# Moving the first head's row maxima into the projection stage, and loading masks instead of computing them, in a one-core decoder layer

## The chip, the core and the metric

The kernel runs on one core of one Trainium2 chip. A core has a matrix engine (PE, with weight loads shown apart as PEld), a vector engine (DVE), an activation engine (ACT), a general engine (POOL) and a queue engine (SP) that only issues transfers here. Each engine works through its own instructions in order. The metric is the device time of the whole kernel in microseconds (us); the profile shows one execution of it, instruction by instruction.

## What is computed

One layer of a decoder over 16 learned meta tokens and 1,024 tokens, 1,024 channels each, in float32:

```python
h = rms_norm(h_res, pre_norm_g[i])
z = h @ w_in[i]                       # one projection, 7,328 columns
(pv, pg, cq, ckv, kr, mg, cu, cg, sbcx, sg, gl) = split_cols(z)
y_a = (pool_mixer(pv, ...) * silu(pg)) @ w_out_pool[i]
y_b = (mla_attention(cq, ckv, kr, ...) * silu(mg)) @ w_out_mla[i]
y_c = (conformer_conv(cu, ...) * silu(cg)) @ w_out_conf[i]
y_d = (short_conv(sbcx, ...) * silu(sg)) @ w_out_sc[i]
gts = sigmoid(gl + gate_bias[i])
m = gts[0] * y_a + gts[1] * y_b + gts[2] * y_c + gts[3] * y_d
h_res = h_res + rms_norm(m @ w_o[i], post_norm_g[i])
```

The attention branch has 8 heads. Queries are made from a normed 256-wide projection, keys and values from a normed 128-wide one; a rotary part of 32 channels is shared by all heads on the side of the keys. Scores are causal, and the softmax runs over all keys up to the query:

```python
s = jnp.einsum('bqhd,bkhd->bhqk', qb, k)
s = jnp.where(k_pos <= q_pos, s, -inf)
p = softmax(s)
o = einsum('bhqk,bkhd->bqhd', p, v)
```

## The kernel before, in words

Products in float32 are made from pairs of rounded halves, a high and a low part, with three matrix products each (high by high, high by low, low by high).

The kernel has three stages, and each is planned and issued by itself (`plan.flush()`, L1282, L1548, L1741).

*Projection.* The large products `h @ w_in` are made in the Strassen-Winograd manner: `unit` (L598) makes seven products of four 128-row blocks, 12 matrix instructions each, in the banks `ps_pa` to `ps_pd`, and writes its results to DRAM (`z_dram`, `th_dram`). `prep` (L567) loads weights, makes their sums on DVE and splits them on ACT and POOL. Beside this run four lanes of side tasks (L1232). A lane is a list of tasks in order, and `pump` (L1244), called after each product, records a step of each lane at the lane's pace. The second lane matters here: it makes the sums of the output weights that the last stage needs (`task_so`, L1200, four times: two loads of 512 KB, four additions and subtractions, two stores), then keys and values (`task_kv`), then queries for each half of the tokens (`task_q`, twice). All of this lane's larger tiles come from one group of four buffers, `t4` (L544); its small weights come from two buffers `w1`; its products go to the two `ps_x` banks. The third lane uses the four buffers `t2`.

*Attention* (from L1288). Head by head and for each half `c` of the queries (512 each), in the order of `seq` (L1492):
- `maxima(h, c)` (L1347) multiplies queries by keys, 128 queries at a time, adds the causal mask `maskS` to the last 128 columns, and reduces each block to row maxima in `mx` and then `mr`. PE transposes `mr`, and DVE multiplies it by a pattern of -1 (`negd`) into four extra rows of the query tile `qt`. The key tile `kt` has four rows of ones there, so that the score product subtracts the maximum by itself.
- `attend(h, c)` (L1380) makes the scores by key blocks with the keys as stationary operand, adds `maskT` where needed, takes the exponential on ACT, splits it on ACT and POOL (`pt`), and multiplies by the values (`vt`) into the bank `ps_o`, which is copied to `ol` (two buffers).
- `sums` and `head_out` normalise a head and gate it.
- `fills` (L1458) gives filler work: the output products of the other three branches (`ps_y`), 48 steps of 6 matrix instructions, each with a gate tile `th` (three buffers) and a weight tile `whl`.

At the head of this stage POOL fills `maskS`, `maskT`, `negd` and the ones rows of both `kt` tiles. `load_kv(0)` and the first two queries are loaded freely. What the loop loads further (L1524), head 1's keys and values included, stands in `plan.behind()`.

*Output.* The attention branch's output products, then `m @ w_o` in the Strassen-Winograd manner, the last norm, and the stores.

*What sets the order.* All code records operations; `Plan.flush` (L351) then plays them through a small model of the engines and issues them in the order that comes out. An operation is taken when its inputs are ready by the model, its tile has a free buffer, and no ready operation of its engine has a lower place. Places follow the order of recording, less `ahead(n)`; `behind()` (L267) lets an operation wait for the last PE operation recorded so far; `slow(n)` adds time to a load's modelled landing. Buffers of a group are given out in the order of recording. A tile of the second stage whose memory lies over tiles of the first waits for the last use of those (`lay_out`, L247). The modelled durations come from `cost` (L291). By the sizes of the tiles, the three `qt` buffers, the last part of `negd` and the first part of `kt0` lie over the four `t4` buffers, and `kt1` over the `t2` buffers.

The helper that issues every operation is one line (L349), so the profile's rows are told apart by tile names.

Of the kernel before, what the change touches and what calls it, by code (L numbers as in the profile page):

```python
# [21 lines left out]
F32 = mybir.dt.float32  # L22
# [26 lines left out]
LK, LR = 1088, 576  # L49

# [162 lines left out]
class Plan:  # L213
# [77 lines left out]
    def cost(eng, op, outs, ins, pow_):  # L291
# [163 lines left out]
def trunk_kernel(ctx, tc, a):  # L455
# [44 lines left out]

    z_dram = {}
# [15 lines left out]
    r_dram = [dram.tile([NT], F32, name=f"r{h}") for h in range(H)]  # L517

# [408 lines left out]

    def task_conv(m, c):
# [203 lines left out]

    def task_kv():
# [84 lines left out]
    def lane(*tasks):  # L1218
# [15 lines left out]
        lane(*[((), task_so, k) for k in range(KH)], (("ckv", "kr"), task_kv), (("cq0", "cq1"), task_q, 0), ((), task_q, 1),  # L1234
# [67 lines left out]
    for d in range(4):  # L1302
# [5 lines left out]
    maskS = qk.tile([P, P], F32, name="maskS")  # L1308
    POOL.memset(maskS, 0.0)
    POOL.affine_select(out=maskS, in_=maskS, compare_op=ALU.is_ge, fill=NEG,  # L1310
                       base=0, pattern=[[-1, P]], channel_multiplier=1)
    maskT = qk.tile([P, P], F32, name="maskT")
    POOL.memset(maskT, 0.0)
    POOL.affine_select(out=maskT, in_=maskT, compare_op=ALU.is_ge, fill=NEG,
                       base=0, pattern=[[1, P]], channel_multiplier=-1)

    negd = qk.tile([4, 4, P], F32, name="negd")
    POOL.memset(negd, -1.0)
    POOL.affine_select(out=negd, in_=negd, compare_op=ALU.is_equal, fill=0.0,
                       base=0, pattern=[[-1, 4], [0, P]], channel_multiplier=1)  # L1320
# [10 lines left out]
    for i in range(2):  # L1331
        POOL.memset(f(kt[i][QK:NA, 0, :L]), 1.0)

    def load_kv(h):
        e, k_, v_ = h % 2, kt[h % 2], vt[h % 2]
        k_ = k_[:, :, :L]
        ld(k_[:64], k_dram[h // 2][64 * e:64 * (e + 1)])
        if h == 0:
            ld(k_[64:96], kr_dram)
        if h == 1:  # L1340
            ld(k_[64:80], kr_dram[16:])
            ld(k_[80:96], kr_dram[:16])
# [4 lines left out]
    def maxima(h, c):  # L1347
# [7 lines left out]
        for r in range(4):  # L1355
# [5 lines left out]
            for b in range(nb):  # L1361
# [3 lines left out]
                if b == nb - 1:  # L1365
                    add(DVE, s[:, n - P:n], s[:, n - P:n], maskS)
# [410 lines left out]
```

## Time and profile before

| what | value |
|---|---|
| median of 3 runs | 1002.54 us (1001.99 to 1002.88) |
| the profiled execution | 1000.41 us |
| its span, first to last instruction | 998.7 us |
| PE busy | 972.7 us, 97% |
| DVE, POOL, ACT busy | 691.4, 690.7, 444.5 us |
| moved by DMA | 200.98 MB, mean 201 GB/s |

The profile gives each engine's busy time, the clock granted to PE, and for each wait what ended it. A row of the timeline is: start, length, engine, line, operation, tile written and tiles read, shapes, count, and in brackets the idle time before it with the operation that ended it. SPq rows are issues of transfers by SP. A row of a group ends with busy time, mean length in ns, and the idle time before it. The row of a wait is: total, times, longest.

### The profile page before, as it was taken

Reading aid. Unit: us, or ns where it says so; the run is one execution under the profiler, and the core shown is the slowest. Engines: PE = TensorE matmul, PEld = TensorE weight load, DVE = VectorE, ACT = ScalarE, POOL = GpSimd, SP = SyncE. Lnnn points to the kernel's source line nnn. Section 1 sums busy time; section 2 is a strip of 40 time slices with the busy share of each in tenths; the row PEclk is TensorE's granted clock in tenths of the full one; section 3 lists DMA queues with packets and bytes.
Section 4 is the critical chain, followed back from the end, with each engine's and each line's share of the span. In section 5 each row is a group of like instructions: output and inputs, shape, how many; then the busy total and the mean of one; then the engine's idle time right before and its main releaser. Section 6 shows DMA issues by size and latency. Waiting matters only on the chain.

```text
span 998.7 us, 15346 instructions
## 1 busy us (share of the span) xinstructions
PE 972.7 (97%) x5093; PEld 826.4 (83%) x5093; DVE 691.4 (69%) x1109; ACT 444.5 (45%) x898; POOL 690.7 (69%) x640
## 2 busy tenths in 40 slices
PE   9999998999999999999999999989999989999996
PEld 9999997889888887888877888868888878688885
DVE  6857979989789545635555464266687787799547
ACT  7643232443335544544534444116665446224631
POOL 6867586776566787776888587225679766656956
PEclk9999999999999999999999999989999999999998
DMA  7258664577877684677655647886649762683534
GB/s 250 76 186 282 213 205 150 164 233 254 261 249 231 227 283 149 212 232 216 187 167 170 205 146 242 295 225 214 190 139 272 194 192 75 242 248 112 187 108 168
DMA packets 133407, 200.98 MB, mean 201 GB/s; under 512 B 20034, under 2 KB 80569, under 8 KB 132560
## 3 DMA queue, kind: packets, MB, share of 16 engines
q1 hardware_dynamic: 124352, 183.22, 58.8%
q10 hardware_dynamic: 8656, 15.74, 4.2%
q8 instruction: 40, 0.66, 0.3%
q0 software_dynamic: 320, 1.05, 0.3%
q14 instruction: 39, 0.32, 0.1%
HBM read 127.31 MB, written 72.65 MB: 200 GB/s over the span
## 4 chain that ended last, share of the span: by engine, by line
PE 86%; POOL 4%; DVE 4%; issue 3%; DMA 2%; ACT 1%; SPq 0%; ACTq 0%; DVEq 0%; POOLq 0%
PE ps_pa L349 15%; PE ps_pb L349 14%; PE ps_pc L349 13%; PE ps_o L349 10%; PE ps_s L349 7%; PE ps_pd L349 7%; PE ps_y L349 7%; PE ps_u L349 7%; PE ps_x L349 4%; POOL S L349 1%; PE ps_w L349 1%; POOL A L349 1%; DMA kt<-kr 1%; DVE m L349 1%; POOL rs L349 1%
## 5 line engine op out<-in xcount | busy, mean ns | idle before, releaser
L349 PE MATMUL ps_pb<-T,S 128*128 128x512 f32 (+2 forms) x792 | 170.7, 359 | 0.0
L349 PE MATMUL ps_pa<-B,A 128*128 128x512 f32 (+2 forms) x792 | 170.0, 359 | 0.0
L349 POOL TENSOR_TENSOR S<-ss,S 128x512 fp32r<-128x512 f32 x84 | 113.7, 1366 | 59.8 <-ACT S L349 57.1
L349 PEld LDWEIGHTS ps_pa<-B,A 128*128 128x128 f32 x792 | 134.0, 188 | 22.1 <-issue 1.0
L349 PEld LDWEIGHTS ps_pb<-T,S 128*128 128x128 f32 x792 | 133.9, 189 | 21.8 <-issue 0.5
L349 POOL TENSOR_TENSOR pt<-p,pt 128x512 fp32r<-128x512 f32 (+4 forms) x112 | 103.5, 950 | 53.5 <-ACT pt L349 28.6
L349 POOL TENSOR_TENSOR A<-raw,A 128x512 fp32r<-128x512 f32 x84 | 112.6, 1350 | 38.9 <-ACT A L349 36.9
L349 DVE TENSOR_TENSOR u<-ps_pb,u 128x512 f32<-128x512 f32 (+2 forms) x66 | 40.3, 610 | 80.4 <-PE ps_pb L349 77.7
L349 DVE SCALAR_TENSOR_TENSOR ps_w<-conv,par,ps_w 128x512 f32<-128x512 f32 x116 | 87.2, 752 | 2.5
L349 PE MATMUL ps_pc<-T,S 128*128 128x512 f32 (+1 forms) x396 | 85.7, 360 | 0.0
L349 ACT ACTIVATE p<-ps_s 128x512 f32<-128x512 f32 (+4 forms) x112 | 49.6, 442 | 80.3 <-PE ps_s L349 35.8
L349 PE MATMUL ps_pd<-T,A 128*128 128x512 f32 (+2 forms) x396 | 84.7, 359 | 0.0
L349 PE MATMUL ps_y<-bo,whl 128*128 128x512 f32 x288 | 83.5, 410 | 0.1
L349 PE MATMUL ps_pc<-B,S 128*128 128x512 f32 (+1 forms) x396 | 83.4, 357 | 0.0
L349 ACT ACTIVATE S<-ss 128x512 fp32r<-128x512 f32 x84 | 50.3, 627 | 66.3 <-DVE ss L349 46.1
L349 PE MATMUL ps_o<-pt,vt 128*128 128x512 f32 (+4 forms) x336 | 73.8, 335 | 2.4 <-ACT ol L349 2.3
L349 PEld LDWEIGHTS ps_pd<-T,A 128*128 128x128 f32 x396 | 67.1, 188 | 10.7
L349 PEld LDWEIGHTS ps_pc<-T,S 128*128 128x128 f32 x396 | 66.5, 189 | 11.1 <-issue 0.7
L349 PEld LDWEIGHTS ps_pc<-B,S 128*128 128x128 f32 x396 | 66.8, 188 | 10.6
L349 PE MATMUL ps_s<-qt,kt 100*128 100x512 f32 (+4 forms) x336 | 68.0, 332 | 0.7 <-DVE qt L349 0.7
L349 PEld LDWEIGHTS ps_o<-pt,vt 128*128 128x128 f32 (+1 forms) x336 | 52.8, 174 | 15.6 <-ACT ol L349 3.6
L349 PEld LDWEIGHTS ps_s<-qt,kt 100*128 100x128 f32 (+1 forms) x336 | 55.7, 182 | 11.8 <-issue 0.9
(265 smaller groups left out, 1913.4 us busy)
## 6 DMA issues: line engine op xcount, KB each, us to landing
raw<-in_w_in_dram SPq DMA_DIRECT2D x52, 512.0 KB
th<-th SPq DMA_DIRECT2D x32, 512.0 KB
th<-z ACTq DMA_DIRECT2D x60, 256.0 KB
v<-vhl SPq DMA_DIRECT2D x16, 384.0 KB
qt<-q SPq DMA_DIRECT2D x16, 384.0 KB
vt<-v SPq DMA_DIRECT2D x8, 768.0 KB
bo<-bo SPq DMA_DIRECT2D x6, 1024.0 KB
kt<-k SPq DMA_DIRECT2D x8, 520.0 KB
```

Source lines behind the costliest of these rows:

```text
L349: getattr(self.handle[o["eng"]], o["op"])(*map(real, o["args"]), **{k: real(v) for k, v in o["kw"].items()})
```

## The change

- The row maxima of head 0 are made in the projection stage: a task `task_first(c)` for each half loads the head's keys and queries from DRAM into `t4` buffers, makes a mask, multiplies and reduces as before, in the `ps_x` banks, and leaves the result in a small tile `mrs`. `maxima` of head 0 in attention only transposes it.
- The masks, the -1 pattern and the ones rows are made once in the projection stage by `task_consts`, stored in DRAM, and loaded at the head of attention.
- In the second lane `task_kv` and `task_q` come first, then `task_consts`, `task_first` twice, and `task_so` last.
- At the first turn of the attention loop, the loads of head 1's keys and of the next query are not `behind` any more; head 1's values stay so. The filler's loads are `behind`, except for the first tile.
- `head_out` of all heads but the last is recorded 450 places later (`ahead(-450)`).
- One tile `mxs`, filled once, takes the place of the `mx` tiles filled for each head and half.
- The model's durations are altered: ACT on PSUM, memsets and `affine_select`, POOL's operations, and DVE's `scalar_tensor_tensor` with source and target in PSUM.

```diff
+FIRST = 1
...
+        psum = any(isinstance(v, View) and v.buf.psum for v in outs + ins)
         if eng == "ACT":
-            return 200 + 0.83 * n, 0
+            return (160 + 0.857 * n if psum else 200 + 0.83 * n), 0
+        if op in ("memset", "affine_select"):
+            return (60 if op == "memset" else 180) + 0.85 * n, 0
         if eng == "POOL":
-            return (500 + 140 * n if pow_ else 80 + 2.4 * n), 0
-        psum = any(isinstance(v, View) and v.buf.psum for v in outs + ins)
+            return (500 + 140 * n if pow_ else 180 + 2.2 * n), 0
         if op == "reciprocal":
             return 150 + 8.5 * n, 0
-        return 142 + (1.2 if op == "scalar_tensor_tensor" and not psum else 1.07) * n, 0
+        both = psum and outs[0].buf.psum
+        return 142 + (1.2 if op == "scalar_tensor_tensor" and (both or not psum) else 1.07) * n, 0
...
+    mrs = const.tile([P, FIRST, 2, 4], F32, name="mrs")
...
+    mask_dram = [dram.tile([P, P], F32, name=f"mask{i}") for i in range(2)]
+    negd_dram = dram.tile([4, 4, P], F32, name="negd")
+    ones_dram = dram.tile([4, L], F32, name="ones4")
...
+    def causal(mask, sign=1):
+
+        POOL.memset(mask, 0.0)
+        POOL.affine_select(out=mask, in_=mask, compare_op=ALU.is_ge, fill=NEG,
+                           base=0, pattern=[[-sign, P]], channel_multiplier=sign)
+
+    def task_consts():
+
+        for i in range(2):
+            mask = w1([P, P], name="mask")
+            causal(mask, 1 - 2 * i)
+            ld(mask_dram[i], mask)
+        t = t4([4, L], name="kone")
+        POOL.memset(t, 1.0)
+        ld(ones_dram, t)
+        t = t4([4, 4, P], name="negd")
+        POOL.memset(t, -1.0)
+        POOL.affine_select(out=t, in_=t, compare_op=ALU.is_equal, fill=0.0,
+                           base=0, pattern=[[-1, 4], [0, P]], channel_multiplier=1)
+        ld(negd_dram, t)
+        yield
+
+    def k_rows(k_, h, part):
+
+        e = h % 2
+        ld(k_[:64], part(k_dram[h // 2][64 * e:64 * (e + 1)]))
+        if h < 2:
+            for r in range(2):
+                ld(k_[64 + 16 * r:80 + 16 * r], part(kr_dram[16 * (r ^ e):16 * (r ^ e) + 16]))
+
+    def row_maxima(c, mx, q_, k_, mask, bank):
+
+        for r in range(4):
+            nk = NM + P * (4 * c + r + 1)
+            nb = -(-nk // 512)
+            w_ = -(-nk // nb)
+            w_ += w_ % 2
+            n0 = 0
+            for b in range(nb):
+                n = min(w_, nk - n0)
+                s = bank()
+                PE.matmul(s[:, :n], q_[:, P * r:P * (r + 1)], k_[:, n0:n0 + n], start=True, stop=True)
+                if b == nb - 1:
+                    add(DVE, s[:, n - P:n], s[:, n - P:n], mask)
+                DVE.tensor_reduce(mx[:, r, b:b + 1], s[:, :n], axis=AX.X, op=ALU.max)
+                n0 += n
+            yield
+
...
+    def task_first(c):
+
+        n = NM + 512 * (c + 1)
+        for h in range(FIRST):
+            k_ = t4([QK, L], F32R, name="k0")[:, :n]
+            k_rows(k_, h, lambda x: x[:, 0, :n])
+            q_ = t4([QK, 512], F32R, name="q0")
+            ld(q_, q_dram[c][h][:, 0])
+            mask = w1([P, P], name="mask")
+            causal(mask)
+            yield
+            mx = tp.tile([P, 4, 3], F32, name="mx")
+            POOL.memset(mx, NEG)
+            yield from row_maxima(c, mx, q_, k_, mask, bank)
+            DVE.tensor_reduce(mrs[:, h, c], mx, axis=AX.X, op=ALU.max)
...
-        lane(*[((), task_so, k) for k in range(KH)], (("ckv", "kr"), task_kv), (("cq0", "cq1"), task_q, 0), ((), task_q, 1),
+        lane((("ckv", "kr"), task_kv), (("cq0", "cq1"), task_q, 0), ((), task_q, 1), ((), task_consts), ((), task_first, 0), ((), task_first, 1),
+             *[((), task_so, k) for k in range(KH)],
              ): 0.9,
...
-    maskS = qk.tile([P, P], F32, name="maskS")
-    POOL.memset(maskS, 0.0)
...
+    mxs = at.tile([P, 2, 2, 4, 3], F32, name="mxs")
+    POOL.memset(mxs, NEG)
+    maskS, maskT = (qk.tile([P, P], F32, name=n) for n in ("maskS", "maskT"))
     negd = qk.tile([4, 4, P], F32, name="negd")
...
-    for i in range(2):
-        POOL.memset(f(kt[i][QK:NA, 0, :L]), 1.0)
+    for t, src in ((maskS, mask_dram[0]), (maskT, mask_dram[1]), (negd, negd_dram),
+                   *((kt[i][QK:NA, 0, :L], ones_dram) for i in range(2))):
+        ld(t, src)
...
-        mx = at.tile([P, 4, 3], F32, tag="mx", bufs=2, name="mx")
-        POOL.memset(mx, NEG)
...
+        if h < FIRST:
+            mr = mrs[:, h, c]
+            for _ in range(4):
+                yield
+        else:
+            mx = mxs[:, h % 2, c]
+            yield from row_maxima(c, mx, q_[:QK, 0], k_[:QK, 0], maskS, lambda: bank("s"))
+            mr = at.tile([P, 4], F32, tag="mr", bufs=2, name="mr")
+            DVE.tensor_reduce(mr, mx, axis=AX.X, op=ALU.max)
...
-                whl = wtile(fp, wname, d, 0)
                 th = fp.tile([P, NT], F32, tag="th", bufs=3, name="th")
-                ld(th, th_dram[8 * gi + d])
+                with plan.behind() if d + bi else nullcontext():
+                    whl = wtile(fp, wname, d, 0)
+                    ld(th, th_dram[8 * gi + d])
...
-        with plan.behind():
+        with plan.behind() if i else nullcontext():
             if i + 2 < len(seq):
                 load_q(*seq[i + 2])
             if c == 0 and h + 1 < H:
                 load_kv(h + 1)
+                if i == 0:
+                    with plan.behind():
+                        load_v(1)
...
-        with plan.ahead(300 if h == H - 1 else 0):
+        with plan.ahead(300 if h == H - 1 else -450):
```

More of the change, by code (lines that the diff above doesn't have):

```diff
@@ L13 @@
 import re
-from contextlib import ExitStack, contextmanager
+from contextlib import ExitStack, contextmanager, nullcontext
 import concourse.bass as bass
@@ L1336, in load_kv, with load_v @@
         k_ = k_[:, :, :L]
-        ld(k_[:64], k_dram[h // 2][64 * e:64 * (e + 1)])
-        if h == 0:
-            ld(k_[64:96], kr_dram)
+        k_rows(k_, h, lambda x: x)
         if h == 1:
-            ld(k_[64:80], kr_dram[16:])
-            ld(k_[80:96], kr_dram[:16])
+            return
+        load_v(h)
+    def load_v(h):
+        v_ = vt[h % 2]
         v = v_dram[h // 4][h % 4]
```

26 lines of the change are left out of this document (removed).

## The prediction

> **What bounds the kernel now.** I read the page first, for the busy shares and the granted clock; then the windows, to find where the matrix engine (PE) loses time; then the chain and the timeline there.
>
> ```profile
> span 998.7 us, 15346 instructions
> PE 972.7 (97%) x5093; PEld 826.4 (83%) x5093; DVE 691.4 (69%) x1109; ACT 444.5 (45%) x898; POOL 690.7 (69%) x640
> PEclk9999999999999999999999999989999999999998
> ```
>
> PE is the bound: busy in 97% of the span, so 26 us idle. The clock row is nearly flat, with a dip about two thirds of the way. The windows (span, each engine's busy time, granted clock, DMA share, GB/s) show both losses at one place, where the projection ends and attention begins:
>
> ```profile
> 50.00:170.00 120.00, 117.61 (x854) 111.53 (x851) 94.62 (x142) 39.66 (x83) 84.89 (x65) 1.00 0.65 210
> 565.00:645.00 80.00, 79.60 (x357) 65.29 (x356) 36.08 (x46) 32.18 (x57) 47.74 (x43) 1.00 0.68 215
> 650.00:660.00 10.00, 9.34 (x43) 7.56 (x43) 6.93 (x15) 0.00 (x0) 0.61 (x4) 1.00 0.84 280
> 660.00:665.00 5.00, 4.63 (x23) 3.21 (x22) 4.97 (x15) 3.54 (x9) 2.49 (x3) 1.00 1.01 215
> 665.00:670.00 5.00, 1.86 (x7) 1.78 (x8) 1.85 (x7) 0.22 (x2) 1.23 (x4) 0.74 1.01 262
> 670.00:675.00 5.00, 5.00 (x19) 4.25 (x18) 2.26 (x6) 0.60 (x1) 0.00 (x0) 0.50 0.14 36
> 675.00:680.00 5.00, 5.00 (x17) 3.97 (x17) 1.98 (x5) 3.52 (x7) 2.25 (x2) 0.74 0.31 105
> ```
>
> Idle: 0.66 + 0.37 + 3.14 = 4.2 us. Half clock: 5 x (0.26 + 0.50 + 0.26) = 5.1 us of lost pace. Together 9.3 us; the projection's last 80 us, for comparison, lose 0.4. The chain there (start, length, what) and the timeline's rows say why:
>
> ```profile
> 641.08 2.72 PE ps_pc L349 x12
> 658.44 8.73 DMA kt<-kr
> 643.64 0.71 PE L349 MATMUL ps_s<-kt,qt 96*128 96x144 f32 x4
> 645.02 12.00 PE L349 MATMUL ps_y<-bo,whl 128*128 128x512 f32 x52
> 648.47 1.87 POOL L349 MEMSET kt<- 4x1040 f32 x2
> 656.07 1.80 DVE L349 TENSOR_REDUCE mx<-ps_s 128x1 f32<-128x144 f32 x5
> 657.85 0.55 SPq L349 DMA_DIRECT2D kt<-k  x1
> 668.14 0.78 PE L349 MATMUL ps_s<-kt,qt 96*128 96x144 f32 x2 [3.22 <-DMA kt<-kr]
> ```
>
> The first head's maxima for its first half are multiplied from 643.64 on but reduced only at 656. PE spends 12 us on filler (the branches' output products). The planner had set the reductions so late because it prices each ones-row memset of `kt` at 80 + 2.4 x 1040 = 2.58 us; the row says 1.87 for two. Head 1's keys are loaded `behind` the last of those maxima, so their DMAs leave at 657.85. Filler and head 0's scores run out at 664.9, and the rotary rows land 8.73 us after issue. The filler is not lost work; the 9.3 us are.
>
> **The change, part by part.** *Maxima of head 0.* Their products have 144+272+400+528 columns for the first half and 656+784+912+1040 for the second, 4,736 in all. At 2.72 us per 12 x 512 that is 2.1 us of PE, which moves and doesn't vanish: 0. DVE takes 14 reductions and 8 mask adds along:
>
> ```profile
> L349 DVE TENSOR_REDUCE mx<-ps_s x112: 300/500/634, 656.1 to 837.3; 128x1 f32<-128x264 f32 x16, 128x1 f32<-128x328 f32 x16, 128x1 f32<-128x392 f32 x16, 128x1 f32<-128x456 f32 x16
> L349 DVE TENSOR_TENSOR ps_s<-ps_s,maskS 128x128 f32<-128x128 f32 x64 | 18.3, 290 | 7.6 <-PE ps_s L349 7.5
> PE ps_x L349 <- POOL rs L349: 2.6, 2, 2.0
> ```
>
> 14 x 0.50 + 8 x 0.29 = 9.3 us, hidden in the projection's last 80 us, where DVE works 36. But PE takes its queue in order, and each product needs one of two `ps_x` banks back from DVE. The nearest row for a side task that is planned too early is the wait for `rs`, 2.6 us; bounds 0 and +2.6. I take +1.0: the 14 steps are short and DVE is half idle.
>
> *Masks, -1 rows and ones rows.* POOL's work for them in front of attention goes (1.87 for the ones rows, and six small instructions). In its place stand, in the projection, four instructions for the two stored masks, four for the masks of the early maxima, three for the row patterns, and four stores; then, for attention, five loads. With eight loads for the early maxima and one more for the rotary rows, that is 18 more DMAs on SP, at 0.3 to 0.6 us of issue (the `kt<-k` row has 0.55): some 8 us of a queue that is mostly empty. POOL's 48 us of 80 leave room. 0, as long as the loads come early; that is the first rival. The 16 memsets of `mx` become one. Five of them held POOL's queue, and with it the splits of the exponentials, behind DVE:
>
> ```profile
> POOL mx L349 <- DVE mr L349: 13.9, 5, 7.6
> PE ps_s L349 <- DVE mr L349: 2.8, 1, 2.8
> PE ps_o L349 <- ACT ol L349: 2.3, 3, 1.6
> 810.02 5.42 DVE L349 TENSOR_TENSOR m<-m,th 128x512 f32<-128x512 f32 x1
> 800.00:820.00 20.00, 16.81 (x86) 13.92 (x86) 16.92 (x28) 7.42 (x20) 14.99 (x18) 0.94 0.70 230
> ```
>
> *Keys and queries of head 1 not behind; its values, and all filler tiles but the first, behind; heads' outputs 450 places later.* Head 1's keys can then leave as soon as their place is free. It lies over the side tasks' `t2` buffers, last read at 612.54 by the store quoted below. That takes the 3.14 us wait and the half clock away. What is late next is the short chain transpose, multiplication by -1 rows, first scores (the 0.66 us above), now with two filler steps and head 1's maxima beside it. I leave 1.0 of the 9.3. The 450 places work on the `ol` buffers (2.3 us of PE waits now): normalising later can hold `ol` longer, or spare DVE a blocked queue. Attention's other big loss is 800 to 820, 3.2 us idle and 0.06 x 20 = 1.2 of clock, behind one DVE addition of 5.42 us. A new order can lose it or repeat it elsewhere: bounds -4.4 and +4.4, and I take 0, as no row says which.
>
> *Prices in the planner.* They cost nothing themselves and alter the order. The convolution's step was priced 142 + 1.07 x 512 = 690 ns and is now 756:
>
> ```profile
> L349 DVE SCALAR_TENSOR_TENSOR ps_w<-conv,par,ps_w 128x512 f32<-128x512 f32 x116 | 87.2, 752 | 2.5
> ```
>
> A plan nearer to the chip should not wait more; counted with the bounds above.
>
> *The output weights' sums (`task_so`) go to the end of their lane.* This frees 40 to 124 us, where PE idles 2.4 us of 120; bounds 0 and -2.4, I take -0.7. What it costs at the other end depends on when the lane ends:
>
> ```profile
> 39.52 1.72 SPq L349 DMA_DIRECT2D so<-in_w_o_dram  x2
> 52.63 0.34 SPq L349 DMA_DIRECT2D so<-in_w_o_dram  x1
> 66.76 0.86 SPq L349 DMA_DIRECT2D so<-in_w_o_dram  x1
> 72.94 0.93 SPq L349 DMA_DIRECT2D so<-in_w_o_dram  x2
> 85.65 0.44 SPq L349 DMA_DIRECT2D so<-in_w_o_dram  x1
> 101.18 0.33 SPq L349 DMA_DIRECT2D so<-so  x1
> 122.50 1.70 SPq L349 DMA_DIRECT2D so<-so  x2
> 129.16 0.92 SPq L349 DMA_DIRECT2D kcs<-in_trig_dram  x2
> 607.52 0.61 SPq L349 DMA_DIRECT2D q<-qr  x1
> 612.54 0.34 SPq L349 DMA_DIRECT2D bo<-cgt  x1
> 614.05 0.57 SPq L349 DMA_DIRECT2D kt<-k  x1
> ```
>
> The lane lives in four `t4` buffers. Its keys got their last buffer at 129.2, after the sums; without them the fourth buffer is there at 66.8. So keys and queries shift by some 62 us, and the last query is stored at about 546 instead of 607.5. The early maxima follow: a load at up to 8.7 us, then 14 blocks at up to 1.3 us (estimate: product, add, reduction, hand-overs), so buffers come free at about 563 and 574. Then the sums, two at a time. The third took 72.9 to 101.5, 28 us, the fourth 85.7 to 124.2, 38 us. In the emptier stretch after 565 (POOL busy 60% against 71%) I put 24 us each, and 5 for a store to land: 574 + 2 x (24 + 5) = 632. Attention's first query, its first keys and the -1 rows lie over the same buffers; loaded then, they are there before PE is done at about 645 (641.08 + 2.72 now, and 2.1 of products moved in, less the small change). So 0 in the forecast, with 10 us to spare.
>
> **Sum.** -9.3 + 1.0 (chain left) + 1.0 (early maxima) + 0 - 0.7 = -8.0 us, on the profiled execution's 1000.4 (span 998.7 and 1.7 around it): 992.4. The median of the runs shown is 2.1 above that execution, so 994.5.
>
> On the size of the half clock the Trainium skill, "TensorE: Matmul & The Clock Gate", Part 1, has a rule: about 3.4 us of sustained work restores full speed. By that rule the dip would cost 1.7 us instead of 5.1 and the sum would be -4.6; the granted clock here says three windows long, so the row decides and the rule gets no chance of its own.
>
> **Rivals.** *1, slower: the sums end too late.* If they keep their old pace of 38 us, the last buffer is free at 574 + 2 x (38 + 5) = 660, and the load of head 0's queries and keys adds 5 more. PE is done at 645 and has only two filler steps (6 x 0.227 us each, 2.7 us in all), since the other filler tiles now wait behind attention. Idle 660 + 5 - 645 - 2.7 = 17 us, and the half clock again 5: +22 against -9.3, some 1015. It decides from about 647 on: 4 us idle and 5 of clock eat the gain. At 652 the time is 1008. For it: the old pace and the DMA share, 0.68 already, to which four sums add 8 MB. Against: the emptier POOL, and a stretch after 625 without weights to prepare.
> The Trainium skill, "SBUF — State Buffer", section on the two separate sides, gives this rival a cause: an addition on DVE with two SBUF inputs and a POOL instruction that reads SBUF shut each other out for a whole instruction. The 5.42 us addition above agrees in kind, though it is longer than one instruction of POOL.
>
> *2, the wait only moves.* With more loads ahead of attention, head 1's keys or another tile land late again, and 4 us idle with 5 of clock stand elsewhere: 1002. For it: a DMA share of 1.01 at 660 to 670. Against: 30 us between 614 and 645 in which the queue can load.
>
> *3, attention gains too.* The 800 to 820 loss goes as well: 994.5 - 4.4 = 990. For it: the 13.9 us of POOL behind `mx`, gone by construction. Against: the 5.42 us addition has no tie to it.
>
> **How the numbers follow.** Forecast (with its own bounds, 991 to 999) 0.54; rival 3 0.10; rival 2 0.10; rival 1 0.26. A change under 0.2% (2 us) can't be told from none here. Faster: 0.54 + 0.10 + 0.02 of rival 2 = 0.66. Same: 0.06 of rival 2. Slower: 0.26 + 0.02 = 0.28. The range 989 to 1008 leaves out the far end of rival 1, about 0.13, and 0.04 below; the forecast alone is 991 to 999.
>
> **What would show it.** Right: the maxima's products of head 0 under `ps_x` before 645; `kt<-k` of head 1 issued before 645; clock 1.00 through 640 to 680; the block of 52 filler products broken up. The sums' last store before 635 and head 0's `kt<-k` before 640 clear rival 1. Wrong: PE idle around 645 on a DMA of `qt`, `kt` or `negd`, with `so<-so` stores just before; new waits of `ps_x` on DVE over 2.6 us in all; waits of `ps_o` on `ol` beyond 2.3.

## The result and the profile after

| | kernel before | changed kernel |
|---|---|---|
| median, us | 1002.31 (1001.99 to 1002.88) | 991.15 (990.20 to 991.64) |
| profiled execution, us | 1000.4 | 990.85 |
| its span, us | 998.7 | 989.0 |

The ratio is 0.9887, with an interval from 0.9870 to 0.9904: 1.1% faster. The time lies inside the predicted range, 3.4 us below the predicted 994.5. The total came out near, but its largest term did not.

The head of the changed kernel's page:

```profile
span 989.0 us, 15388 instructions
PE 969.4 (98%) x5095; PEld 824.6 (83%) x5095; DVE 696.8 (70%) x1109; ACT 444.0 (45%) x898; POOL 692.7 (70%) x630
```

PE idles 19.6 us of the span; before it was 26.0. The windows of the changed kernel (span, busy time of PE, PEld, DVE, ACT, POOL, then granted clock, DMA share, GB/s):

```profile
50.00:170.00 120.00, 117.99 (x874) 113.07 (x873) 84.34 (x135) 46.10 (x98) 76.45 (x62) 1.00 0.56 168
565.00:645.00 80.00, 79.62 (x358) 65.35 (x356) 47.09 (x56) 30.52 (x48) 54.52 (x41) 1.00 0.79 246
645.00:650.00 5.00, 1.16 (x6) 0.52 (x4) 1.46 (x3) 0.72 (x1) 0.00 (x0) 1.00 1.01 423
650.00:655.00 5.00, 5.00 (x19) 4.23 (x20) 3.31 (x12) 2.73 (x6) 2.61 (x4) 0.53 1.01 408
655.00:660.00 5.00, 5.00 (x22) 4.00 (x20) 0.00 (x0) 1.77 (x6) 1.75 (x4) 0.78 1.04 339
660.00:680.00 20.00, 20.00 (x117) 17.03 (x116) 13.93 (x39) 12.58 (x30) 12.43 (x14) 1.00 0.71 227
```

The hole at the start of attention is still there. It now lies at 645 to 650 instead of 660 to 670: 3.84 us idle and 5 x (0.47 + 0.22) = 3.45 us of pace lost to half clock, 7.3 together, where the prediction had counted 9.3 before. Only 2.0 of the 8.3 us came. The timelines of the changed kernel's PE, DVE and POOL (start, length, engine, and in brackets the idle time before and what ended it) show the wait that took the old one's place:

```profile
643.69 1.29 PE L353 MATMUL ps_pc<-B,S 128*128 128x512 f32 x5
645.40 0.47 PE L353 MATMUL ps_s<-kt,qt 96*128 96x144 f32 x2 [0.20 <-PE ps_s L353]
649.25 0.45 PE L353 MATMUL ps_s<-kt,qt 96*128 96x400 f32 x1 [3.38 <-DVE z L353]
648.50 0.69 DVE L353 TENSOR_TENSOR z<-ps_pc,u 128x512 f32<-128x512 f32 x1 [8.23 <-DMA th<-z]
649.23 1.28 DVE L353 TENSOR_TENSOR qt<-ps_s,negd 4x512 fp32r<-4x512 f32 x2
639.34 0.76 POOL L353 DMA_DIRECT2D th<-z  x1 [11.35 <-ACT z L353]
```

The projection's last gate block needs one of three `z` buffers back. The store out of that buffer was issued on POOL at 639.34 and lands some 9 us later, so DVE stands 8.23 us, until 648.50. Behind the waiting instruction on DVE's queue is the multiplication of head 0's maxima by `negd`, and behind that all scores of attention. The DMA share is 1.01 to 1.04 there; POOL's four gate stores took 6.7 to 9.0 us to land, in the kernel before 3.7 to 6.7. The SP queue of the changed kernel says why the transfers bunch:

```profile
617.75 0.43 SPq L353 DMA_DIRECT2D maskS<-mask  x1
618.23 0.42 SPq L353 DMA_DIRECT2D maskT<-mask  x1
619.85 0.27 SPq L353 DMA_DIRECT2D negd<-negd  x1
622.16 2.49 SPq L353 DMA_DIRECT2D kt<-ones  x2
626.03 0.54 SPq L353 DMA_DIRECT2D kt<-k  x1
631.42 1.25 SPq L353 DMA_DIRECT2D kt<-kr  x2
```

The five small loads stand ahead of head 0's keys, and the queue stops among them. Its waits from 610 to 640 (total, times, longest) name the gate stores `th<-z`, from which these loads read nothing:

```profile
SPq L353 <- DMA th<-z: 10.2, 4, 4.8
```

The trace's record of the semaphores shows what ties them. The 678 transfers that SP and ACT issue take eight semaphores in turn to tell of their landing, and one starts only when the one that had its semaphore before has landed. Four stores of ACT landed at 622.14, 624.34, 626.01 and 631.40; the four loads that have their semaphores next (the two of the ones rows, `kt<-k` and the first `kt<-kr`) left at 622.16, 624.40, 626.03 and 631.42. POOL's stores have semaphores of their own. This belongs to the program, and the planner knows of it: `fits` in `Plan.flush` lets no transfer of SP or ACT start while the eighth before it is in flight.

`kt<-k` leaves at 626.03; before it left at 614.05. After 631 everything goes at once.

So where did the 9.7 us of span go? The output stage starts here, in the kernel before and in the changed one:

```profile
868.10 2.10 PE L349 MATMUL ps_u<-boM,whl 128*128 128x512 f32 x8
```

```profile
859.29 2.09 PE L353 MATMUL ps_u<-boM,whl 128*128 128x512 f32 x8
```

The projection ended at 641.08 + 2.72 = 643.8 and now ends at 643.69 + 1.29 = 645.0: +1.2, though 2.1 us of products moved in. Attention took 868.1 - 643.8 = 224.3 and now takes 859.3 - 645.0 = 214.3: -10.0, of which 2.1 are those products, 2.0 the smaller hole, and 5.9 lie in its later part. The rest of the span gave 0.9. The later part of attention in the windows, before and after:

```profile
720.00:800.00 80.00, 79.30 (x427) 66.22 (x426) 61.95 (x149) 46.33 (x103) 66.97 (x71) 1.00 0.71 197
800.00:870.00 70.00, 64.61 (x330) 52.24 (x330) 54.90 (x101) 32.06 (x73) 46.88 (x46) 0.98 0.50 171
```

```profile
720.00:800.00 80.00, 80.00 (x424) 66.27 (x422) 56.73 (x141) 41.10 (x93) 62.29 (x61) 1.00 0.77 214
800.00:860.00 60.00, 58.61 (x300) 47.23 (x300) 47.36 (x91) 25.82 (x59) 40.43 (x37) 1.00 0.54 173
```

Idle and clock before: 0.70 + 5.39 + 0.02 x 70 = 7.5 us. After: 1.39. These 6.1 us are the term that the prediction took as 0.

### The profile page after: what moved, and what is told of

The parts are those of the page before. It is cut to its first block, busy times and chain, and to the rows that moved or that the text cites. A ratio compares the mean times of both kernels' runs of the same rounds, so it can differ in the third digit from the quotient of the medians.

```text
span 989.0 us, 15388 instructions
## 1 busy us (share of the span) xinstructions
PE 969.4 (98%) x5095; PEld 824.6 (83%) x5095; DVE 696.8 (70%) x1109; ACT 444.0 (45%) x898; POOL 692.7 (70%) x630
## 5 line engine op out<-in xcount | busy, mean ns | idle before, releaser
L353 POOL TENSOR_TENSOR A<-raw,A 128x512 fp32r<-128x512 f32 x84 | 114.6, 1370 | 39.2 <-ACT A L353 37.6
L353 POOL TENSOR_TENSOR pt<-p,pt 128x512 fp32r<-128x512 f32 (+4 forms) x112 | 105.6, 967 | 49.4 <-PE ps_s L353 31.5
L353 PE MATMUL ps_y<-bo,whl 128*128 128x512 f32 x288 | 87.1, 409 | 0.0
L353 PE MATMUL ps_pc<-B,S 128*128 128x512 f32 (+1 forms) x396 | 86.4, 359 | 0.0
L353 PE MATMUL ps_s<-qt,kt 100*128 100x512 f32 (+4 forms) x336 | 70.5, 333 | 0.3 <-DVE qt L353 0.3
L353 DVE TENSOR_TENSOR z<-ps_pc,u 128x512 f32<-128x512 f32 (+1 forms) x66 | 40.2, 609 | 37.3 <-PE ps_pc L353 27.3
```

Source lines behind the costliest of these rows:

```text
L353: getattr(self.handle[o["eng"]], o["op"])(*map(real, o["args"]), **{k: real(v) for k, v in o["kw"].items()})
```

## The experiments

The theories: *the pile-up* says that the hole at the start is caused by the order of the loads, so that removing one wait there shows another until the loads are spread. *The shut-out* says that the later part gained because a DVE instruction with both inputs in SBUF no longer stands for several us behind POOL. Against them stand the prediction's mechanism, the early maxima, and the single edits: places, prices, order of the sums. The kernel before had medians of 1000.2 to 1001.8 us beside these runs; the ratios are against it. The changed kernel itself was measured only in the first comparison (991.15, ratio 0.9887), so a difference of about 2 us from it by medians tells nothing.

**The last gate block without the wait for a `z` buffer.** The result goes into the block's own temporary tile.

```diff
-    def halves_of(n, each, store):
+    def halves_of(n, each, store, own=None):
...
-            z = up.tile([P, n], F32, tag="z", bufs=3, name="z")[:m, :nj]
+            z = tmp if (i, j) == own else up.tile([P, n], F32, tag="z", bufs=3, name="z")[:m, :nj]
...
-        return halves_of(512, each, lambda i, j, t: (POOL if g == 30 else ACT).dma_start(half(th_dram[g + i], j), t))
+        return halves_of(512, each, lambda i, j, t: (POOL if g == 30 else ACT).dma_start(half(th_dram[g + i], j), t),
+                         (0, 1) if g == 30 else None)
```

> The changed kernel, but the projection's very last gate block is made in the tile u2, which nobody needs any more, so that it doesn't wait for one of the three z buffers. Theory A (DVE stands at 645 to 648.5 in front of this block because a gate store issued at 639 has not landed, and head 0's multiplication by -1 rows is queued behind it): PE's 3.4 us wait and the 6.8 us of half clock after it both go, 3.4 + 3.4 = 6.8 us, so about 984.5. Rival (the DMA queues are simply full at 640 to 660, and keys or queries would be late anyway): PE waits for a tile of qt or kt in the same place, and the time stays at 989 to 991.

Measured 992.82 us, ratio 0.9893 to 0.9931. The 3.38 us wait is gone, and PE's waits in attention begin with

```profile
PE ps_y L353 <- DMA whl<-w_out_pool: 3.7, 1, 3.7
```

at 653: a filler's weights. From 645 to 660 PE loses 4.45 us idle and 3.45 of pace, no less than in the changed kernel (3.84 and 3.45). The named wait was only the first of several, and the time is above both expectations.

**Without the -450.** Heads' outputs are recorded in their old places.

```diff
-        with plan.ahead(300 if h == H - 1 else -450):
+        with plan.ahead(300 if h == H - 1 else 0):
```

> The changed kernel with the heads' outputs recorded at their old place (0 instead of -450). Attention after its first 35 us lost 7.3 us less than before; theory B gives this to the later place of the outputs: then the loss comes back, about 998. Rivals (prices, the single mx tile, filler spared at the start): within 1.5 us of 991.

Measured 998.10 us, 0.9950 to 0.9974: 7 us of the gain are lost. The start is as in the changed kernel; the loss lies at 807. The longest of DVE's rows there, PE's second wait in attention, and the product that it holds up:

```profile
802.41 4.57 DVE L353 TENSOR_TENSOR op<-ol,rb 64x512 f32<-64x512 f32 x2
```

```profile
PE ps_s L353 <- DMA whl<-w_out_sc: 2.8, 1, 2.8
807.65 0.27 PE L353 MATMUL ps_s<-ident,mr 128*4 128x128 f32 x1 [2.82 <-DMA whl<-w_out_sc]
```

One of the two multiplications took 3.96 us. The profile names the weights' load as releaser, but the matrix product that waits is the transpose of `mr`, which the row-maximum chain behind that DVE row feeds; `mr` is reduced at 806.90.

**The old prices in the changed kernel.** The planner's cost function is that of the kernel before.

```diff
-            return (160 + 0.857 * n if psum else 200 + 0.83 * n), 0
+            return 200 + 0.83 * n, 0
-        if op in ("memset", "affine_select"):
-            return (60 if op == "memset" else 180) + 0.85 * n, 0
...
-            return (500 + 140 * n if pow_ else 180 + 2.2 * n), 0
+            return (500 + 140 * n if pow_ else 80 + 2.4 * n), 0
...
-        return 142 + (1.2 if op == "scalar_tensor_tensor" and (both or not psum) else 1.07) * n, 0
+        return 142 + (1.2 if op == "scalar_tensor_tensor" and not psum else 1.07) * n, 0
```

> The changed kernel with the planner's old durations. Theory C (better prices made attention's order better): 5 to 7 us slower than 991. Rivals: within 2 us, and the stalls of the projection move by a microsecond or two.

Measured 997.95 us, 0.9950 to 0.9981. The changed prices are worth some 7 us within the changed kernel. The loss lies in several places: the half clock at the start lasts 10.2 us instead of 6.8, and attention's later part has three waits of 0.7 to 0.8 us and several of 0.3. One DVE addition is long again, though PE's wait behind it, at 826, is only 0.7 us:

```profile
821.75 3.95 DVE L350 TENSOR_TENSOR m<-m,th 128x512 f32<-128x512 f32 x1
```

**The sums of the output weights first again.**

```diff
-        lane((("ckv", "kr"), task_kv), (("cq0", "cq1"), task_q, 0), ((), task_q, 1), ((), task_consts), ((), task_first, 0), ((), task_first, 1),
-             *[((), task_so, k) for k in range(KH)],
+        lane(*[((), task_so, k) for k in range(KH)], (("ckv", "kr"), task_kv), (("cq0", "cq1"), task_q, 0), ((), task_q, 1), ((), task_consts), ((), task_first, 0), ((), task_first, 1),
```

> The changed kernel with the output weights' sums first in their lane again. By the forecast's reckoning the lane then ends 60 us later: last query stored near 595, early maxima done near 635, and head 0's tiles, which lie over the same buffers, are loaded from 635 to 640 on and land near 645: 2 to 8 us slower than the changed kernel, 993 to 999. Rival: the sums' place doesn't matter, or the emptier queue at 640 lets the gate store land in time: 984 to 991.

Measured 996.59 us, 0.9903 to 0.9958, five runs from 992.37 to 997.50, so its size is not certain; it is not better. The projection ends 2 us later than in the changed kernel, with the wait for `rs` at 166 back (2.1 us, and half clock behind it). A wait of 2.1 us at 767 is new. Attention's start keeps its hole (a wait of 3.4 us for `qt`): the sums at the end of the lane were not what made the start crowded.

**The small loads behind the large ones.** The loop of five loads is recorded after `load_kv(0)` and the queries.

```diff
-    for t, src in ((maskS, mask_dram[0]), (maskT, mask_dram[1]), (negd, negd_dram),
-                   *((kt[i][QK:NA, 0, :L], ones_dram) for i in range(2))):
-        ld(t, src)
...
     load_kv(0)
     load_q(*seq[1])
+    for t, src in ((maskS, mask_dram[0]), (maskT, mask_dram[1]), (negd, negd_dram),
+                   *((kt[i][QK:NA, 0, :L], ones_dram) for i in range(2))):
+        ld(t, src)
     lead_to(0)
```

> The changed kernel with the five small loads (two masks, the -1 rows, two of ones rows) issued behind head 0's keys, values and second query instead of ahead of them. Theory D: a load on SP waits for the landing of the eighth transfer before it, so the five small loads hold the keys from 617 to 626 and 631 while the DMA engines are half idle; the large loads then pile up at 635 to 660, and the projection's last gate stores land late. Then here the keys leave before 622, the DMA share falls below 1 at 645 to 655, and PE's 3.4 us wait and the 6.8 us of half clock go: 984 to 986. Rival E (the sums of the output weights, moved next to the end of the projection, bring too many bytes there whatever the order): the pile and a wait of 3 us or more stay, 989 to 993.

Measured 988.93 us, 0.9868 to 0.9928: 2 us below the changed kernel by the medians, 1 above by the ratios (0.9898 to 0.9887), so the two are not told apart, and the theory's 984 to 986 was not reached. Its queue and PE's first wait in attention:

```profile
616.25 0.54 SPq L353 DMA_DIRECT2D kt<-k  x1
616.84 2.22 SPq L353 DMA_DIRECT2D kt<-kr  x2
```

```profile
PE ps_s L353 <- DMA bo<-bo: 1.8, 1, 1.8
```

The keys leave 9.8 us earlier, and the stall halves from 3.38 to 1.79. What is left is the same wait for `z`, whatever the row names: DVE stands 6.21 us for a gate store, until 645.03, its addition ends at 645.72, and the product starts at 645.78; the load of `bo` lands in that same tenth of a microsecond. Half clock still follows, 6.8 us of it. The gate stores still hold SP for 8.7 us in three waits, now ahead of later loads.

**Masks, patterns and ones computed in place, with all else changed.** `task_consts` also leaves its lane.

```diff
-    for t, src in ((maskS, mask_dram[0]), (maskT, mask_dram[1]), (negd, negd_dram),
-                   *((kt[i][QK:NA, 0, :L], ones_dram) for i in range(2))):
-        ld(t, src)
+    causal(maskS)
+    causal(maskT, -1)
+    POOL.memset(negd, -1.0)
...
+    for i in range(2):
+        POOL.memset(f(kt[i][QK:NA, 0, :L]), 1.0)
```

> The changed kernel without the stored patterns: POOL makes masks, -1 rows and ones rows at the head of attention, as in the kernel before. Theory D: keys and queries leave by 620 and the pile at 640 to 660 is smaller; but POOL comes to the patterns only behind its last gate store at 645 or later, and head 0's scores need the ones rows, some 4 us of memsets: PE waits for POOL instead, 1 to 4 us, 987 to 992. Theory F (loading the masks is itself a gain of several us): 994 or more.

Measured 990.97 us, 0.9884 to 0.9947: the same as the changed kernel by the medians, up to 3 us slower by the ratios (0.9916 to 0.9887), with intervals that overlap. The long wait falls to 1.2 us (for `qt` on DVE), but half clock lasts 10.2 us: the start loses some 7 us as in the changed kernel, though the keys leave at 613.89. POOL makes the patterns at 646.5 to 650.6, behind its last gate store. Whether loading them is a small gain or none is not shown.

**The -450 alone, in the kernel before.**

```diff
-        with plan.ahead(300 if h == H - 1 else 0):
+        with plan.ahead(300 if h == H - 1 else -450):
```

> The kernel before with one edit, the heads' outputs recorded 450 places later. Theory B (this edit alone takes the loss of late attention away): the waits at 800 to 850 go, 5 to 7 us faster than before, 995 to 997. Rival (it works only with the spared filler or the single mx tile): 1000 to 1003.

Measured 1004.93 us, 1.0027 to 1.0066: slower, the opposite of its sign in the changed kernel. The shut-out is still there,

```profile
813.45 4.65 DVE L349 TENSOR_TENSOR m<-m,th 128x512 f32<-128x512 f32 x1
```

with a wait of 2.9 us for the row maxima at 819 behind it.

**The new prices alone, in the kernel before.** The reverse of the price edit above.

> The kernel before with one edit, the planner's new durations. Theory C: attention's and the projection's stalls shrink, 4 to 7 us faster than before, 995 to 998; the memsets of ones rows are then planned short, so the first head's maxima are reduced earlier and the filler at 645 shrinks. Rival (prices matter only where the rest of the change makes the plan tight): 1000 to 1003.

Measured 998.33 us, 0.9959 to 1.0006, ten runs from 994.36 to 1003.58: unclear, at best a small gain. The profiled execution has no wait over 0.5 us between 644 and 800 and no half clock there, but 6.8 us of half clock at 167. From 645 to 690 PE idles 2.7 us, where the kernel before loses 9.3: a block of 24 filler products stands in the place of the block of 52, and head 1's keys, still `behind`, leave at 652.64 instead of 657.85. So in this profile the prices alone take most of the old hole away, without the early maxima and without unbinding the keys. The gain does not show clearly in the medians, and no run separates the memsets' price from the others.

**The changed kernel without the early maxima.** Head 0's maxima are made in attention.

```diff
-FIRST = 1
+FIRST = 0
...
-        lane((("ckv", "kr"), task_kv), (("cq0", "cq1"), task_q, 0), ((), task_q, 1), ((), task_consts), ((), task_first, 0), ((), task_first, 1),
+        lane((("ckv", "kr"), task_kv), (("cq0", "cq1"), task_q, 0), ((), task_q, 1), ((), task_consts),
```

> The changed kernel with FIRST = 0: the six products per half and the twelve row maxima of head 0 are made in attention again, from scores of the loaded keys, as in the kernel before; the sums still stand behind keys and queries, masks and the row of ones are still loaded, prices and the -450 stay. The recorded prediction's mechanism (the early maxima take a chain of about 9 us out of the start of attention): about 8 us slower than the changed kernel, 999 us, with the first 35 us of attention losing 8 us more than the 10.3 of the changed kernel. The rival that the traces of the other runs speak for (the wait only moved, since the loads of the start come late either way and another wait ends last): the projection is 1 to 2 us shorter, the start of attention about 1 to 3 us longer, 990 to 993 us. If the first stretch loses over 15 us, the early maxima are worth what was predicted and were only paid away by the small loads; if it loses 10 to 12, they are worth about nothing.

Measured 996.45 us, 0.9928 to 0.9966, between the two expectations: the early maxima are worth 5.3 us by the medians and 3.2 by the profiles. PE's waits from 640 to 690:

```profile
PE ps_s L353 <- DVE z L353: 4.2, 1, 4.2
PE ps_s L353 <- DVE mxs L353: 1.5, 1, 1.5
PE ps_s L353 <- DVE qt L353: 1.1, 2, 0.8
PE ps_y L353 <- DMA whl<-w_out_pool: 0.9, 1, 0.9
```

The `z` wait stands here too, so it doesn't come from the early maxima. From the end of the projection to 690 PE loses 7.7 us idle and 5.1 of pace (10.2 us of half clock), in the changed kernel 3.8 and 3.4: the early maxima are worth 5.6 us at the start, and 0.8 of idle time behind 690. The projection ends at 640.7 without them instead of 645.0. Of these 4.3 us, 1.3 lie ahead of 80 us, where the early maxima have not begun (the first wait for `u` ends at 79.41 here and at 80.71 there), and the same 1.3 to 1.5 separate the changed kernel from runs with the same projection (the small loads late: 79.31 and 643.5). So the early maxima cost the projection 3.0 us, 2.1 of them the products.

**The third branch's additions on POOL, in the kernel before.**

```diff
-                        add(POOL if bi == 1 else DVE, m_[c][d], m_[c][d], t)
+                        add(POOL, m_[c][d], m_[c][d], t)
```

> The kernel before with the 16 additions of the third branch (m<-m,th, two inputs in SBUF) on POOL instead of DVE; nothing else is edited, though the planner may order its neighbours anew. In the kernel before one of them took 5.42 us at 810.02 while POOL ran instruction after instruction, and TensorE then stood 2.84 us and ran 3.4 us at half clock. Theory (the gain in the later part of attention is that no DVE addition is shut out there any more): no DVE instruction over 2 us between 800 and 830, the gap at 816.5 and the half clock behind it are gone, attention 4 to 5 us shorter, 995 to 998 us. Rival (the row-maximum chain of the last heads is late for another reason, or POOL with 16 x 1.27 us more work becomes the bound): a gap over 2 us remains between 800 and 860 with no long DVE instruction ahead of it, 1000 to 1005 us.

Measured 998.67 us, 0.9954 to 0.9996, between the two expectations. The 5.42 us addition, the 2.84 us gap at 816.5 and the half clock behind it are gone:

```profile
800.00:820.00 20.00, 20.00 (x110) 16.86 (x109) 15.43 (x34) 11.20 (x28) 19.64 (x22) 1.00 0.67 209
820.00:870.00 50.00, 46.26 (x226) 37.01 (x225) 26.20 (x51) 21.84 (x48) 47.80 (x45) 0.93 0.47 158
```

In the kernel before, 800 to 820 lost 3.2 us idle and 1.2 of clock. All of it comes back: from 800 to 870 the kernel before loses 6.8 us and this run 7.2 (3.75 idle and 0.05 x 70 of clock). The largest piece is at 862, behind two multiplications of the last head (the first takes 2.95 us) that run while POOL makes six additions without a break:

```profile
858.02 3.55 DVE L349 TENSOR_TENSOR op<-ol,rb 64x512 f32<-64x512 f32 x2
861.50 1.27 DVE L349 SCALAR_TENSOR_TENSOR th<-th,ps_y 128x512 f32<-128x512 f32 x2
```

```profile
852.94 7.48 POOL L349 TENSOR_TENSOR m<-m,th 128x512 f32<-128x512 f32 x6
```

PE then waits 2.2 us for `th`. The instruction that is shut out has changed, its victim too, but the picture is the same. The profiled execution's span is 2.6 us shorter than that of the kernel before. That is no more than the shorter half clock at 670 gives (3.4 instead of 10.2 us, so 3.4 us of pace), and this has no tie to the edit.

**Both edits at the start: small loads late, and the own tile.** The edits are those shown above.

> The changed kernel with both edits that took something off its start: the five small loads behind the keys and queries (989 alone) and the last gate block's result written into its own temporary tile instead of one of three z buffers (removed the 3.38 us wait, but 993 alone, since a weight load was late next). Theory (the waits at the start are the pile-up of transfers, and the own tile matters only once that is thinned out): the gap at the start falls below 1 us, no half clock at 646, 985 to 988 us. Rival (the next wait, on the biases or a weight, takes the place again): a gap of 1.5 to 3.5 us with half clock behind it remains, 988 to 993 us.

Measured 989.17 us, 0.9859 to 0.9890. No wait over 0.4 us is left at the start and no half clock: from the projection's end to 660 PE loses 0.8 us, where either edit alone left 5.5 (late loads) and 7.9 (own tile). So the pile-up and the `z` wait had both to go. Yet the median is that of the late loads alone, not 985 to 988. Its later part has an `op` multiplication of 3.05 us at 801.7, with no wait over 0.4 us behind it; where the gain went was not found.

**The same with the gate stores of the last two gate blocks on POOL.**

```diff
-        return halves_of(512, each, lambda i, j, t: (POOL if g == 30 else ACT).dma_start(half(th_dram[g + i], j), t),
+        return halves_of(512, each, lambda i, j, t: (POOL if g >= 28 else ACT).dma_start(half(th_dram[g + i], j), t),
```

> As the run with small loads late and the own tile, and the gate stores of the last two blocks but one (th from 28 on, the last four pairs of stores) issued by POOL too instead of ACT, so that fewer gate stores stand in the queue of ACT among which loads wait. Theory (the ring of transfers in flight delays the loads at the start): the first weight and bias loads land earlier and the start loses 1 to 2 us less than the run without it, 984 to 988 us. Rival (POOL's own issue of 0.7 us each and its additions delay the converts it makes for the last blocks; the transfers are the same bytes in the same stretch): the same or up to 3 us slower, 987 to 992 us.

Measured 986.29 us (984.83 to 990.55), 0.9826 to 0.9881: the lowest median of the study, though its interval overlaps those of the two runs with the small loads late and of the changed kernel. The windows around the start:

```profile
615.00:635.00 20.00, 20.00 (x90) 16.55 (x89) 5.75 (x7) 6.47 (x11) 11.01 (x11) 1.00 0.96 216
635.00:645.00 10.00, 10.00 (x47) 8.11 (x46) 3.26 (x5) 2.63 (x4) 1.63 (x3) 1.00 1.02 414
645.00:650.00 5.00, 5.00 (x29) 4.25 (x28) 4.29 (x14) 3.19 (x8) 2.40 (x4) 1.00 0.67 272
```

The changed kernel's row for the first stretch is

```profile
615.00:635.00 20.00, 20.00 (x90) 16.57 (x89) 7.03 (x8) 7.14 (x11) 10.38 (x8) 1.00 0.56 154
```

so the DMA engines were 44% idle there while the loads that were needed stood in SP's queue. With the small loads late the share is 0.79, with the own tile beside it 0.81, and SP still waits 7.6 us for `th<-z`. With the stores on POOL, outside the eight semaphores, no such wait is among SP's, the share is 0.96, and PE has no wait at all from 640 to 690. The hole of 7.3 us is gone, of which the run before had already taken all but 0.8 and small waits behind 660. The medians show 4.9 (991.15 to 986.29), the ratios 3.3 (0.9887 to 0.9854). A wait of 2.1 us stands at 756 in this kernel, behind a held `op` multiplication of 2.75.

## Why the prediction was right, and where it was wrong

*The time* was right, 991.15 against 994.5 and a range from 989 to 1008, but by two errors of opposite sign: the hole at the start came out 6.3 us worse than forecast, the later part of attention 6.1 better. That they cancel is luck.

*"That takes the 3.14 us wait and the half clock away. I leave 1.0 of the 9.3"*: this step failed. It gave 2.0 instead of 8.3. What was said of the old hole held: the 52-product filler block is broken up, and the wait for `kt<-kr` is gone; the run with the prices alone agrees that the late reductions came from the planner's prices, and shows that the early maxima were not the only way. But the second rival, that the wait only moves, held at this place (3.84 us idle and 3.45 of pace, against the 4 and 5 that it gave). The main reason is the step on the masks, *"a queue that is mostly empty ... 0, as long as the loads come early"*. It counted the issue time of the added transfers, 0.3 to 0.6 us each, and not that a load in this queue waits for the transfer that had its semaphore before, here a store of ACT (10.2 us in four waits). The first small loads took the free places, and the keys met those waits. Moving the small loads back took 9.8 us off the keys' issue and 1.8 us off the hole (7.3 to 5.5); with the last gate block out of the `z` buffers as well 0.8 was left. The wait for a `z` buffer, the second cause, stands nowhere in the prediction. What I should have asked of the trace before is the waits of the SP queue: between 610 and 640 the kernel before has

```profile
SPq L349 <- DMA th<-z: 7.0, 1, 7.0
```

*"Bounds -4.4 and +4.4, and I take 0"* for 800 to 820: mis-sized. The changed kernel has there

```profile
800.00:820.00 20.00, 20.00 (x102) 16.27 (x102) 16.17 (x36) 11.07 (x27) 19.69 (x18) 1.00 0.52 165
```

so this stretch gave the full -4.4, and 1.7 more came from its neighbours (a wait of 1.6 us for `ol` at 850 is 0.4 now). The third rival was right in its result. Its reason was not: the runs with the memsets of `mx` gone lose again in the later part where the -450 is taken out (998.10) or, less, the old prices put in (997.95; 3.6 us idle between 690 and 870 against 1.4). Every wait over 2 us in the later part of attention, in the kernel before and the runs without the -450, with the sums first, with the -450 alone, with the additions on POOL and with the last edit, ends 4 to 7 us after the start of a DVE instruction of 2.7 to 5.4 us with both inputs in SBUF. The changed kernel, the small loads late and the masks computed have no such instruction and no such wait. The run with the additions on POOL took the long addition away, and 800 to 820 became whole, while another pair met at 862. But a long instruction is not enough: 3.95 us with the old prices, 3.07 in the run with the own tile and 3.05 in that with both edits had no wait over 0.8 us behind them. What is not settled is why the new order avoids the coincidence: neither the -450 nor the prices were shown to do it alone. So the later gain is in part argued. The coincidence fits the rule of the Trainium skill, "SBUF — State Buffer", section on the two separate sides, on the port that DVE and POOL share, which the prediction weighed, except that the instruction lasts for longer than one of POOL's; no run here measures the port by itself.

*Early maxima, +1.0 on the path*: PE's waits of the changed kernel from 50 to 645 are

```profile
PE ps_pb L353 <- DVE u L353: 2.0, 2, 1.5
PE ps_y L353 <- POOL rs L353: 0.5, 2, 0.4
```

with nothing on `ps_x`, and 565 to 645 loses 0.38 us, as before. The size of the term held: by the run without them they cost the projection 3.0 us, 0.9 beyond the products.

*Sums out of 40 to 124 us, -0.7*: PE's idle there fell by 0.4 (120 - 117.99 against 120 - 117.61). The wait for `rs` at 165.7 went, but one for `u` at 80.7 came.

*The lane's reckoning, with the sums stored at 632*, was on the safe side. The changed kernel's rows:

```profile
531.02 0.62 SPq L353 DMA_DIRECT2D q<-qr  x1
570.07 0.17 DVE L353 TENSOR_REDUCE mrs<-mx 128x4 f32<-128x12 f32 x1
610.88 1.71 SPq L353 DMA_DIRECT2D so<-so  x2
```

The last query store, of the rotary part, left at 531 (546 was said), the early maxima done at 570 (574), the sums' last stores issued by 612.6 (632). The first rival, on which 0.26 stood, never came near its point of 647.

*The parts do not add up.* Taking single parts back costs 7.0 (the -450), 6.8 (prices), 5.4 (sums) and 5.3 (early maxima) by the medians, 24.5 together (4 to 8 each by the ratios), where the whole change is worth 11.2; alone in the kernel before, the -450 costs 3 to 7 us. With a planned order each edit reshuffles what coincides with what, and much of these numbers may be that.

## What to carry to other kernels

When a wait at a stage's start is removed, list every transfer that is to land in that stretch, in queue order, and read the queue's own waits and the DMA share before it: a share of 0.56 ahead of one of 1.02 says that loads are held, not that bandwidth is short. Then ask which semaphore a held load waits for, and which transfer had it before: a store of another engine can stand in the same round. Put small loads that are needed late behind the large ones that are needed first. When a row names a releaser that the waiting product has no use for, look at the weight load of the same product and at DVE's rows. Where two engines that hinder each other both have a run of work, look for single instructions several times their usual length just ahead of a long wait of the bound engine, and move one of the two elsewhere.

## What was not expected of the hardware

- SP's queue waited four times, 10.2 us in all, for stores that ACT had issued and that the loads have no data in common with. The tie is not one of the hardware but of the program's eight semaphores, which the transfers of both queues share; POOL's stores have others, and with four more stores on POOL the waits ended.
- A DVE addition that takes 0.69 to 0.76 us in the median of its kernel took 5.42, 4.65 and 3.95 us. Beside it POOL ran not one instruction but several back to back; in the kernel before, from 810.02 to 815.4, these were

```profile
810.03 2.41 POOL L349 TENSOR_TENSOR pt<-p,pt 128x400 fp32r<-128x400 f32 x4
812.40 2.48 POOL L349 TENSOR_TENSOR m<-m,th 128x512 f32<-128x512 f32 x2
```

- The granted clock's record shows half clock in pieces of 3.41, 6.83 and 10.24 us. The gap of PE ahead of it doesn't fix the length: 3.22 us was followed by 10.24, 3.38 by 6.83, 1.79 by 6.83, 2.84 by 3.41. A gap of 1.97 us at 166 gave none in the kernel before and 6.83 in the kernel with the additions on POOL; 2.12 gave none in the fastest kernel. The 3.4 us that the Trainium skill, "TensorE: Matmul & The Clock Gate", Part 1, gives for the return to full speed is the size of one piece; the runs show up to three. What a wait costs in clock could not be foretold from its length to better than some 5 us of pace (half of 10.24).
